# A matmul with a decayed running sum: a quarter of the weights by another queue, new engine orders for the first 40 slots, four input buffers

## The chip, the cores and the metric

The kernel runs on one core of a Trainium2 chip. The metric is the device time of that core in microseconds; the kernel before takes 908.82 us (median of three, 908.58 to 909.28). The profiled execution took 909.17 us, of which the profile covers 907.1 us from the first instruction to the last.

## What is computed

```python
B, S, D = (16, 2048, 1024)          # x: B x S x D, w: D x D, decay: D, all float32
xw = x @ w
out[:, 0, :] = xw[:, 0, :]
for t in range(1, S):
    out[:, t, :] = decay[None, :] * out[:, t - 1, :] + xw[:, t, :]
```

A matrix product of 32768 x 1024 with 1024 x 1024, and then, along the time axis of each batch, a first-order recurrence with one decay factor for each column.

## The kernel before

x is cut into 64 chunks of 512 time steps. GpSimd's queue loads a chunk as bf16 (four transfers, one for each 32 partitions), VectorE turns it in 32x32 blocks so that the summed dimension lies on the partitions ("T"), and ScalarE reorders it into `xt` ("X", "Y"). TensorE multiplies in bf16, eight matmuls (k = 0 to 7) for 128 output columns by 512 time steps. Two chunks make a group; a slot is one group and one of its eight column blocks, so a group has eight slots, and there are 264 slots: the last two chunks are each a group of their own. A slot's result is a "tile" of 128 columns by 1024 time steps, two PSUM banks.

A tile is emptied in one of two ways. Directly: VectorE scans all 1024 steps out of PSUM. Paired: ScalarE copies PSUM ("p") and makes decay times the even steps ("g"), GpSimd adds them to the odd steps ("j"), VectorE scans only 512 steps with the squared decay, ScalarE and GpSimd fill in the other 512 ("h", "c"). `flips` says for which slots the usual choice (every fourth direct) is turned round. Then VectorE transposes the tile back ("B") and SyncE's queue stores four tiles at a time.

The order on each engine is the order in which the program issues. For the first and last slots it is spelled out in `agenda`, a list of letters with numbers; `deeds` says what each letter does. The key -99 is what comes before slot 0.

```python
    def load(c, q, j0=0, j1=NJ):
        b, t0 = chunks[c]
        if c not in xb_of:
            xb_of[c] = ring(sb, "xb", 3, [128, NJ, CQ], BF16)
        pin(nc.gpsimd.dma_start(
            out=xb_of[c][quad(q), j0:j1],
            in_=_ap(x, [[D, P], [P * D, j1 - j0], [1, CQ]],
                    (b * S + t0 + j0 * P) * D + q * CQ)))

    def turn(c, j0=0, j1=NJ, m0=0, m1=M):
        if c not in xw_of:
            xw_of[c] = ring(sb, "xw", 2, [128, M, NJ, P, 2], BF16)
        src = xb_of[c][:, j0:j1].rearrange("p j c -> p (j c)").bitcast(FP32)
        dst = xw_of[c].rearrange("p m j i e -> p (m j i e)").bitcast(FP32)
        pin(nc.vector.transpose(
            out=dst.rearrange("p (m j i) -> p j m i", m=M, i=P)[:, j0:j1, m0:m1],
            in_=src.rearrange("p (j m c) -> p j m c", m=M, c=P)[:, :, m0:m1]))

# ... (cut)
        def pair(self):
            if self.paired:
                self.copy()
                self.odd()
                self.zero()
                self.join()
# ... (cut)
        def scan(self):
            T, n, so = self.T, self.n, self.so
            if self.paired:
                pin(nc.vector.tensor_tensor_scan(
                    out=so[:, 3:T + 2:2],
                    data0=squares[-1][:, n:n + 1].to_broadcast([128, T // 2]),
                    data1=self.xs[:, 1:T:2],
                    initial=0.0 if self.prev is None else self.prev,
                    op0=ALU.mult,
                    op1=ALU.add,
                ))
            else:
                parts = self.ps if isinstance(self.ps, tuple) else (self.ps,)
                size = T // len(parts)
                for i, ps in enumerate(parts):
                    self.run(ps, i * size, size)

# ... (cut)
    room = [ot_tile(2 * NJ).rearrange("p j c -> p (j c)") for _ in range(2)]
    size = M * CH
    stage = {(0, 0, 0): room[0][:, 0:size // 2],
             (0, 0, M // 2): room[0][:, size // 2:size * 3 // 4].bitcast(BF16),
             (0, 1, 0): room[0][:, size:size * 3 // 2].bitcast(BF16),
             (1, 0, 0): room[1][:, 0:size // 2].bitcast(BF16),
             (1, 1, 0): room[1][:, size // 2:size].bitcast(BF16)}

    def load_w(queue, h, e, m0=0, m1=M):
        for q in range(NQ):
            pin(queue.dma_start(
                out=stage[h, e, m0][quad(q)].rearrange("p (m d) -> p m d", m=m1 - m0),
                in_=_ap(w, [[2 * D, P], [2 * P * D, m1 - m0], [1, CH]],
                        (q * CQ + m0 * 2 * P + e) * D + h * CH)))

    def settle(h, e, m, copy):
        m0 = M // 2 if (h, e) == (0, 0) and m >= M // 2 else 0
        src = stage[h, e, m0][:, (m - m0) * CH:(m - m0 + 1) * CH]
        pin(copy(out=wcols[:, 2 * m + e, h],
                 in_=src.rearrange("p (q r i) -> p q r i", q=NQ, r=R)))

# ... (cut)
    load_w(nc.sync, 0, 0, 0, M // 2)          # first quarter of w, float32
# ... (cut)
    def load_part(i):
        load_w(nc.gpsimd, *((0, 0, M // 2, M), (0, 1), (1, 0), (1, 1))[i])

    def part_one(i, copy):
        part(i // 8, copy, i % 4, i % 4 + 1, *halves[i // 4 % 2])

    def settle_one(i, copy):
        settle(i // 8, i // 4 % 2, i % 4, copy)

# ... (cut)
        -99: "M0 M1 U0 U1 M2 M3 U2 U3 W0 w1 L E0 F0 G1 E1 L F2 D G3 E2 F4 L G5 W2 E3 F6 w3 G7 W4 W6 w5 w7 E4 F8 G9 E5 F10 G11 E6 F12 G13 E7 F14 G15 W8 W10 W9 W11",
        0: "P0 L w15 w13",
        1: "L L L S0 C0",
        2: "L P2 P1 w12 S1 L L B0 B1 S2",
        3: "w14 C2 T2",
        4: "S3 P4 X2 Y2 T3 C1",
# ... (cut)
    flips = (0, 1, -19, -18, -16, -11, -8, -6, -3, -2)
# ... (cut)
            for j0, j1 in halves:                    # chunk 0
                for k in (0, 2):
                    for i in range(R):
                        matmul(firsts[i], i, k, xt_of[0], j0 * P, j1 * P)
            for k in (4, 6, 1, 3, 5, 7):
                for i in range(R):
                    matmul(firsts[i], i, k, xt_of[0])
            # ... then chunk 1 in halves of 256 steps
```

The letters of the head: M loads half a chunk, U a quarter of w, E turns a quarter of chunk 0 or 1 (half its steps, half its columns), F and G copy a piece of it into `xt` on VectorE or ScalarE, W and w copy a piece of w into `wsb` on VectorE or ScalarE, D makes the decay factors, L loads a quarter of a later chunk.

Of the kernel before, what the change touches and what calls it, by code (L numbers as in the profile page):

```python
# [10 lines left out]
BF16 = mybir.dt.bfloat16  # L11
# [14 lines left out]
def kernel(  # L26
# [74 lines left out]
    def load(c, q, j0=0, j1=NJ):  # L101
        b, t0 = chunks[c]
        if c not in xb_of:
            xb_of[c] = ring(sb, "xb", 3, [128, NJ, CQ], BF16)
        pin(nc.gpsimd.dma_start(  # L105
            out=xb_of[c][quad(q), j0:j1],
            in_=_ap(x, [[D, P], [P * D, j1 - j0], [1, CQ]],
                    (b * S + t0 + j0 * P) * D + q * CQ)))
# [152 lines left out]
    class Outlet:  # L261
# [7 lines left out]
        def store(self, b, t0):  # L269
# [3 lines left out]
            for i, q in enumerate((0, 2, 1, 3)):  # L273
# [7 lines left out]
    room = [ot_tile(2 * NJ).rearrange("p j c -> p (j c)") for _ in range(2)]  # L281
    size = M * CH
    stage = {(0, 0, 0): room[0][:, 0:size // 2],
             (0, 0, M // 2): room[0][:, size // 2:size * 3 // 4].bitcast(BF16),
             (0, 1, 0): room[0][:, size:size * 3 // 2].bitcast(BF16),
             (1, 0, 0): room[1][:, 0:size // 2].bitcast(BF16),
             (1, 1, 0): room[1][:, size // 2:size].bitcast(BF16)}
# [25 lines left out]
    for q in range(NQ):  # L313
        pin(nc.sync.dma_start(
            out=rows[q * P:q * P + R],
            in_=_ap(decay, [[P, R], [CH, 2], [1, P]], q * CR)))
    cols = const.tile([128, 2, P], FP32, name="cols")

    def load_half(i):
# [35 lines left out]
    def ending(i):  # L355
        b, t0 = chunks[-1]
        nb = TL // 128
        pts = [ring(psp, name, count, [128, R, 128])
               for name, count in (("spare1", 1), ("ps", 3), ("ps", 3), ("spare", 1))]
        wides = [ring(sb, *spot, [128, NQ, R, P])  # L360
                 for spot in (("xb", 3), ("xb", 3), ("xb", 3), ("h", 4))]

        def cross(blocks, rs):
            for i in blocks:
                for r in rs:
                    t = 2 + i * 128
                    pin(nc.tensor.transpose(  # L367
                        out=pts[i][:, r], in_=tiles[r - R].so[:, t:t + 128], identity=ident))

        def leave(i, copy):  # L370
            pin(copy(out=wides[i].rearrange("p q r i -> p r q i"),
                     in_=pts[i].rearrange("p r (q i) -> p r q i", q=NQ)))
            pin(nc.sync.dma_start(
                out=_ap(out, [[D, 128], [1, CH]], (b * S + t0 + i * 128) * D + CH),
                in_=wides[i].rearrange("p q r i -> p (q r i)")))

        cross((0,), range(R))
        cross((1,), range(R))
        cross((2, 3), range(R - 1))
        cross((2, 3), (R - 1,))  # L380
        for i in range(nb):
            leave(i, (nc.scalar.copy, nc.vector.tensor_copy)[i % 2])
# [2 lines left out]
    slots += [([c], n) for c in groups[-1] for n in range(K)]  # L385
    tiles = []

    def turn_and_load(c):
        turn(c)
        if 2 <= c < nch - 3:  # L390
            loads.extend((c + 3, q) for q in range(NQ))

    loads = [(c, q) for c in (2, 3, 4) for q in range(NQ)]
    deeds = {
        "P": lambda s: tiles[s % len(slots)].pair(),
        "S": lambda s: tiles[s % len(slots)].scan(),
        "C": lambda s: tiles[s % len(slots)].complete(),
        "B": lambda s: tiles[s % len(slots)].back(),
        "T": turn_and_load,
        "X": lambda c: part(c, nc.scalar.copy, 0, 2),  # L400
        "Y": lambda c: part(c, nc.scalar.copy, 2, M),
        "x": lambda c: part(c, nc.vector.tensor_copy, 0, 2),
# [21 lines left out]
        "L": lambda i: load(*loads.pop(0)) if loads else None,  # L424
    }
    agenda = {
        -99: "M0 M1 U0 U1 M2 M3 U2 U3 W0 w1 L E0 F0 G1 E1 L F2 D G3 E2 F4 L G5 W2 E3 F6 w3 G7 W4 W6 w5 w7 E4 F8 G9 E5 F10 G11 E6 F12 G13 E7 F14 G15 W8 W10 W9 W11",
        0: "P0 L w15 w13",
        1: "L L L S0 C0",
        2: "L P2 P1 w12 S1 L L B0 B1 S2",  # L430
        3: "w14 C2 T2",
        4: "S3 P4 X2 Y2 T3 C1",
        5: "",
        6: "L L P5 L B3 L L S4 L S5 B2 C3 X3 Y3 C4 T4",
        7: "P6 C5 S7 X4 S6",
        8: "C7 C6 L d P8 B4 B7 B6",
        9: "B5 P9",
        10: "L S8 P10 C8 T5 X5 L S9",
        11: "L L S11 L C9 Y4 S10 C10 B8",
        12: "",  # L440
        13: "B11 P12 B10 B9 Y5 S12 P13 C12",
        14: "L P14 T6 S13 C13 L Y6 L",
        15: "L S15 L S14 C14",
        16: "B13 B12 B15 B14 P16 X6",
        -20: "z-20",
        -19: "p-20 g-20",
        -18: "j-20 S-19 S-20 k-19 B-19",
# [15 lines left out]
        -2: "S-3 S-4",  # L463
        -1: "S-2 h-4 c-4 a-1 b-1 V",
    }
    flips = (0, 1, -19, -18, -16, -11, -8, -6, -3, -2)
    later = {10: ["Y4"]}
    for c in range(5, nch):
        first = c // 2 * K
        ahead = (7, 6, 4) if c % 2 else (11, 10, 8)  # L470
        for letter, a in zip("TXY", ahead):
            later.setdefault(first - a, []).append(f"{letter}{c}")

    def usual(s):
        paired = [t.paired for t in tiles]
# [25 lines left out]
    for step, (g, n) in enumerate(slots):  # L501
# [7 lines left out]
        if step == 0:  # L509
# [1 line left out]
            firsts = [ps[:, 0:TL] for ps in heads] + [spares[0]]  # L511
            seconds = [ps[:, TL:T] for ps in heads] + [spares[1]]
            for j0, j1 in halves:
                for k in (0, 2):
                    for i in range(R):
                        matmul(firsts[i], i, k, xt_of[0], j0 * P, j1 * P)
            for k in (4, 6, 1, 3, 5, 7):
                for i in range(R):
                    matmul(firsts[i], i, k, xt_of[0])
            for k0 in range(0, K, 4):  # L520
# [6 lines left out]
        if step < R:  # L527
            ps = heads[n] if n < 3 else tuple(spares)
        else:
            if len(g) == 2 or n % R < 3:  # L530
                ps = ring(psp, "ps", 3, [128, T])
            else:
                ps = ring(psp, "spare", 1, [128, TL])
# [1 line left out]
            if step < K:  # L535
                todo.sort(key=lambda kl: kl[0] % 2)
            elif step == K:
                todo.sort(key=lambda kl: kl[1])
            if left == -1:
                ps = tuple(both[:, t:t + TL // 2] for t, both in zip(  # L540
                    (0, TL // 2), (ps, ring(psp, "ps", 3, [128, TL]))))
# [44 lines left out]
```

## Time and profile before

| what | value |
|---|---|
| median of three | 908.82 us |
| span of the profile | 907.1 us |
| TensorE clock granted | 1.000 |
| VectorE, ScalarE, GpSimd busy | 829.7, 680.3, 655.5 us |
| GpSimd's queue (loads, cast to bf16) | 68.96 MB |
| SyncE's queue (stores, first quarter of w) | 134.76 MB |
| HBM read and written | 138.42 and 134.22 MB |

Busy time of an engine is not its worth on the path: TensorE's matmuls are pipelined, and in the profile they show as busy for 377 ns each though one starts about every 216 ns. In the group lines and the timeline, a row is: start and length in us, engine, line of the kernel, operation, what it writes and reads, count, and in brackets the idle time before it with what ended that.

### The profile page before, as it was taken

How to read it: one execution, taken by the hardware profiler on the slowest of the kernel's cores; microseconds unless marked ns; L12 is line 12 of the kernel's file. 1: busy time of each engine (PE TensorE's matmuls, PEld its weight loads, DVE VectorE, ACT ScalarE, POOL GpSimd, SP SyncE). 2: the span in 40 equal slices, each digit the busy share in tenths (PEclk: the TensorE clock that was granted, in tenths of full speed). 3: DMA queues.
4: the chain of work that ended last, by engine and by line, in shares of the span. 5: the costliest groups of instructions: out<-in, count | busy, mean ns of one | idle time of the engine just before them, and what ended most of it. 6: DMA issues, size and time to landing. Idle time of an engine off the chain costs nothing.

```text
span 907.1 us, 12011 instructions
## 1 busy us (share of the span) xinstructions
PE 895.3 (99%) x4187; PEld 409.9 (45%) x4187; DVE 829.7 (91%) x620; ACT 680.3 (75%) x940; POOL 655.5 (72%) x754
## 2 busy tenths in 40 slices
PE   7999999999999999999999999999999999999998
PEld 3544444444444444444444444444444444444444
DVE  4999999999999999999999999999999999999998
ACT  3787887877777778778778777787787787787743
POOL 7777978777777777677686776777777777776632
PEclk9999999999999999999999999999999999999999
DMA  9999999999999999999999999999999999999868
GB/s 163 180 226 237 215 217 249 250 251 254 253 250 243 225 230 234 224 228 232 224 234 221 232 228 226 238 226 225 236 227 228 224 238 223 223 229 217 177 144 237
DMA packets 402605, 204.48 MB, mean 225 GB/s; under 512 B 8817, under 2 KB 401777, under 8 KB 402545
## 3 DMA queue, kind: packets, MB, share of 16 engines
q1 hardware_dynamic: 265200, 134.76, 60.1%
q0 software_dynamic: 137344, 68.96, 56.7%
q8 instruction: 32, 0.52, 0.2%
q14 instruction: 29, 0.23, 0.1%
HBM read 138.42 MB, written 134.22 MB: 301 GB/s over the span
## 4 chain that ended last, share of the span: by engine, by line
PE 94%; DMA 2%; ACT 1%; DVE 1%; POOL 1%; issue 0%; DVEq 0%; POOLq 0%
PE ps L126 93%; DMA xb<-in_x_dram 1%; ACT xt L123 1%; PE spare L126 1%; DMA ot<-in_w_dram 1%; DVE so L216 0%; POOL ot L291 0%; ACT h L164 0%; ACT xs L178 0%; POOL xb L105 0%; DVE ot L253 0%; DVE so L196 0%; PE spare L367 0%; DVE wsb L299 0%; PE ps L367 0%
## 5 line engine op out<-in xcount | busy, mean ns | idle before, releaser
L126 PE MATMUL ps<-xt,wsb 128*128 128x512 bf16 (+1 forms) x4086 | 878.0, 377 | 5.1 <-DVE xt L123 2.8
L126 PEld LDWEIGHTS <-wsb 128*128 128x128 bf16 x4144 | 405.3, 98 | 485.7 <-issue 4.8
L191 POOL TENSOR_TENSOR xs<-h,xs 128x512 f32<-128x512 f32 (+1 forms) x188 | 240.8, 1281 | 200.4 <-ACT h L164 96.4
L178 ACT COPY xs<-ps 128x1024 f32<-128x1024 f32 (+1 forms) x188 | 187.7, 998 | 156.4 <-PE ps L126 154.6
L253 DVE STREAM_TRANSPOSE ot<-so 128x1024 f32<-128x1024 f32 (+1 forms) x260 | 299.7, 1191 | 0.8
L241 POOL TENSOR_TENSOR so<-h,xs 128x512 f32<-128x512 f32 (+1 forms) x188 | 240.0, 1277 | 38.1 <-ACT h L164 21.4
L123 ACT COPY xt<-xw 128x2048 bf16<-128x2048 bf16 (+1 forms) x132 | 240.7, 1825 | 9.8 <-DVE xw L115 9.8
L105 POOL DMA_DIRECT2D xb<-in_x_dram x264 | 174.4, 662 | 1.9 <-POOLq L570 0.9
L164 ACT ACTIVATE h<-so,dec 128x512 f32<-128x512 f32 (+1 forms) x188 | 144.2, 767 | 29.5 <-DVE so L196 26.0
L115 DVE STREAM_TRANSPOSE xw<-xb 128x2048 f32<-128x2048 f32 (+1 forms) x70 | 147.4, 2105 | 6.8 <-DMA xb<-in_x_dram 6.8
L196 DVE TENSOR_TENSOR_SCAN so<-spare,keep,xs 128x512 f32<-128x512 f32 (+1 forms) x96 | 119.4, 1244 | 28.2 <-POOL xs L191 27.9
L196 DVE TENSOR_TENSOR_SCAN so<-spare,xs 128x512 f32<-128x512 f32 x88 | 107.5, 1222 | 27.8 <-POOL xs L191 24.9
L164 ACT ACTIVATE h<-ps,dec 128x512 f32<-128x512 f32 (+1 forms) x188 | 129.0, 686 | 0.0
L216 DVE TENSOR_TENSOR_SCAN so<-dec,ps 128x1024 f32<-128x1024 f32 x35 | 79.0, 2260 | 0.6 <-ACT h L164 0.6
L216 DVE TENSOR_TENSOR_SCAN so<-dec,keep,ps 128x1024 f32<-128x1024 f32 (+1 forms) x36 | 77.1, 2143 | 0.1
L245 ACT COPY keep<-so 128x1 f32<-128x1 f32 x136 | 25.6, 188 | 12.4 <-DVE so L216 12.4
L187 ACT COPY so<-keep 128x1 f32<-128x1 f32 x96 | 18.3, 190 | 1.9 <-DVE ot L253 1.9
L126 PE MATMUL spare<-xt,wsb 128*128 128x512 bf16 (+1 forms) x58 | 12.3, 328 | 0.0
L185 POOL MEMSET so<- 128x1 f32 x92 | 10.7, 116 | 1.1 <-ACT keep L245 1.1
L291 POOL DMA_DIRECT2D ot<-in_w_dram x16 | 8.7, 543 | 3.3 <-DMA xb<-in_x_dram 1.8
L309 PE MATMUL spare<-idle 128*128 128x512 bf16 x27 | 7.6, 451 | 2.3 <-ACT idle L307 2.3
L299 ACT COPY wsb<-ot 128x512 bf16<-128x512 bf16 x7 | 4.0, 616 | 5.5 <-DMA ot<-in_w_dram 5.5
(32 smaller groups left out, 32.9 us busy)
## 6 DMA issues: line engine op xcount, KB each, us to landing
out_dram<-ot SPq DMA_DIRECT2D x248, 512.0 KB, 10.5
xb<-in_x_dram POOLq DMA_DIRECT2D x248, 256.0 KB, 7.7
out_dram<-ot SPq DMA_DIRECT2D x12, 256.0 KB, 4.3
xb<-in_x_dram POOLq DMA_DIRECT2D x16, 128.0 KB, 5.5
ot<-in_w_dram POOLq DMA_DIRECT2D x12, 128.0 KB, 5.0
out_dram<-xb SPq DMA_DIRECT2D x3, 256.0 KB
ot<-in_w_dram SPq DMA_DIRECT2D x4, 128.0 KB, 3.4
ot<-in_w_dram POOLq DMA_DIRECT2D x4, 64.0 KB, 4.5
```

The lines of the kernel that those rows point to most:

```text
L105: pin(nc.gpsimd.dma_start(out=xb_of[c][quad(q), j0:j1], in_=_ap(x, [[D, P], [P * D, j1 - j0], [1, CQ]], (b * S + t0 + j0 * P) * D + q * CQ)))
L115: pin(nc.vector.transpose(out=dst.rearrange("p (m j i) -> p j m i", m=M, i=P)[:, j0:j1, m0:m1], in_=src.rearrange("p (j m c) -> p j m c", ...
L123: pin(copy(out=xt_of[c][:, m0:m1, :, j0 * P:j1 * P], in_=src))
L126: pin(nc.tensor.matmul(out=ps[:, t0:t1] if ps.shape[1] >= t1 else ps, lhsT=wsb[:, k, n].rearrange("p q i -> p (q i)"), rhs=xt[:, k // 2, k ...
L164: pin(nc.scalar.activation(out=h, in_=src, func=mybir.ActivationFunctionType.Copy, scale=dec[:, self.n:self.n + 1]))
L178: pin(nc.scalar.copy(out=self.xs, in_=self.ps))
L191: pin(nc.gpsimd.tensor_tensor(out=odds, in0=self.g, in1=odds, op=ALU.add))
L196: pin(nc.vector.tensor_tensor_scan(out=so[:, 3:T + 2:2], data0=squares[-1][:, n:n + 1].to_broadcast([128, T // 2]), data1=self.xs[:, 1:T:2 ...
L216: pin(nc.vector.tensor_tensor_scan(out=so[:, t + 2:t + 2 + size], data0=dec[:, n:n + 1].to_broadcast([128, size]), data1=ps, initial=befor ...
L241: pin(nc.gpsimd.tensor_tensor(out=self.so[:, 2:T + 2:2], in0=self.h, in1=self.xs[:, 0:T:2], op=ALU.add))
L245: pin(nc.scalar.copy(out=self.keep, in_=self.so[:, self.T + 1:self.T + 2]))
L253: pin(nc.vector.transpose(out=outlet.ot[:, :, c0:c0 + P], in_=self.so[:, 2 + t0:2 + t0 + nj * P].rearrange("p (i t) -> p i t", t=P)))
```

## The change

The second quarter of w (even rows, first half of the columns, upper half of the summed dimension) is loaded by SyncE's queue as float32, as the first quarter is, and no longer by GpSimd's queue with a cast to bf16; the room for it in SBUF was there. In return the third quarter stands right behind chunk 0 in GpSimd's queue. Chunk 0 is multiplied in four k by halves of its time steps and not two, so that the first 32 matmuls need only even rows of w. The orders of all engines are spelled out for slots 0 to 41 and not only 0 to 16, other tiles are direct, chunk 2 is turned and chunk 3 is turned in two pieces, and slots 8 and 9 use chunk 2 for both before either uses chunk 3. The input has four buffers and not three, and loads run four chunks ahead. All this is meant to let TensorE run without gaps from an early time on.

```diff
--- before.py
+++ after.py
@@ -101,7 +101,7 @@
     def load(c, q, j0=0, j1=NJ):
         b, t0 = chunks[c]
         if c not in xb_of:
-            xb_of[c] = ring(sb, "xb", 3, [128, NJ, CQ], BF16)
+            xb_of[c] = ring(sb, "xb", 4, [128, NJ, CQ], BF16)
         pin(nc.gpsimd.dma_start(
             out=xb_of[c][quad(q), j0:j1],
             in_=_ap(x, [[D, P], [P * D, j1 - j0], [1, CQ]],
@@ -281,7 +281,7 @@
     room = [ot_tile(2 * NJ).rearrange("p j c -> p (j c)") for _ in range(2)]
     size = M * CH
     stage = {(0, 0, 0): room[0][:, 0:size // 2],
-             (0, 0, M // 2): room[0][:, size // 2:size * 3 // 4].bitcast(BF16),
+             (0, 0, M // 2): room[0][:, size // 2:size],
              (0, 1, 0): room[0][:, size:size * 3 // 2].bitcast(BF16),
              (1, 0, 0): room[1][:, 0:size // 2].bitcast(BF16),
              (1, 1, 0): room[1][:, size // 2:size].bitcast(BF16)}
@@ -314,6 +314,7 @@
         pin(nc.sync.dma_start(
             out=rows[q * P:q * P + R],
             in_=_ap(decay, [[P, R], [CH, 2], [1, P]], q * CR)))
+    load_w(nc.sync, 0, 0, M // 2, M)
     cols = const.tile([128, 2, P], FP32, name="cols")
 
     def load_half(i):
@@ -358,7 +359,7 @@
         pts = [ring(psp, name, count, [128, R, 128])
                for name, count in (("spare1", 1), ("ps", 3), ("ps", 3), ("spare", 1))]
         wides = [ring(sb, *spot, [128, NQ, R, P])
-                 for spot in (("xb", 3), ("xb", 3), ("xb", 3), ("h", 4))]
+                 for spot in (("xb", 4), ("xb", 4), ("xb", 4), ("h", 4))]
 
         def cross(blocks, rs):
             for i in blocks:
@@ -385,18 +386,28 @@
     slots += [([c], n) for c in groups[-1] for n in range(K)]
     tiles = []
 
-    def turn_and_load(c):
-        turn(c)
-        if 2 <= c < nch - 3:
-            loads.extend((c + 3, q) for q in range(NQ))
-
-    loads = [(c, q) for c in (2, 3, 4) for q in range(NQ)]
+    def turn_half(half):
+        def act(c):
+            if half == 0:
+                turn(c, 0, NJ, 0, 2)
+            else:
+                turn_and_load(c, 2)
+        return act
+
+    def turn_and_load(c, m0=0):
+        turn(c, 0, NJ, m0, M)
+        if 2 <= c < nch - 4:
+            loads.extend((c + 4, q) for q in range(NQ))
+
+    loads = [(c, q) for c in (2, 3, 4, 5) for q in range(NQ)]
     deeds = {
         "P": lambda s: tiles[s % len(slots)].pair(),
         "S": lambda s: tiles[s % len(slots)].scan(),
         "C": lambda s: tiles[s % len(slots)].complete(),
         "B": lambda s: tiles[s % len(slots)].back(),
         "T": turn_and_load,
+        "t": turn_half(0),
+        "u": turn_half(1),
         "X": lambda c: part(c, nc.scalar.copy, 0, 2),
         "Y": lambda c: part(c, nc.scalar.copy, 2, M),
         "x": lambda c: part(c, nc.vector.tensor_copy, 0, 2),
@@ -424,24 +435,49 @@
         "L": lambda i: load(*loads.pop(0)) if loads else None,
     }
     agenda = {
-        -99: "M0 M1 U0 U1 M2 M3 U2 U3 W0 w1 L E0 F0 G1 E1 L F2 D G3 E2 F4 L G5 W2 E3 F6 w3 G7 W4 W6 w5 w7 E4 F8 G9 E5 F10 G11 E6 F12 G13 E7 F14 G15 W8 W10 W9 W11",
-        0: "P0 L w15 w13",
-        1: "L L L S0 C0",
-        2: "L P2 P1 w12 S1 L L B0 B1 S2",
-        3: "w14 C2 T2",
-        4: "S3 P4 X2 Y2 T3 C1",
-        5: "",
-        6: "L L P5 L B3 L L S4 L S5 B2 C3 X3 Y3 C4 T4",
-        7: "P6 C5 S7 X4 S6",
-        8: "C7 C6 L d P8 B4 B7 B6",
-        9: "B5 P9",
-        10: "L S8 P10 C8 T5 X5 L S9",
-        11: "L L S11 L C9 Y4 S10 C10 B8",
-        12: "",
-        13: "B11 P12 B10 B9 Y5 S12 P13 C12",
-        14: "L P14 T6 S13 C13 L Y6 L",
-        15: "L S15 L S14 C14",
-        16: "B13 B12 B15 B14 P16 X6",
+        -99: "M0 M1 U1 M2 M3 U2 U3 W0 w1 D W2 w3 E1 E0 G2 G3 F1 F0 E2 E3 G4 G5 F7 F6 W6 w7 W4 W5 E5 E4 G10 F11 G9 F8 E6 E7 L G12 F13 L G15 F14",
+        0: "L W9 w11 L W8 W10 L",
+        1: "S0 L",
+        2: "L p1 z1",
+        3: "L w13 S2 w15 k0 L w14 w12 g1",
+        4: "L B0 k2 j1 B2 p4 L S1 L g4",
+        5: "j4 t2 k1 h1 u2 L X2 c1 S3 Y2 z4 L",
+        6: "L L B1 k3 p5 B3 p6 z5 z6 L",
+        7: "g6 S4 g5 L j6 t3 h4 k4 u3 c4 X3 S6 L Y3 L T4 j5 h6 k6 p7 S5 z7 c6 g7",
+        # ... (slots 8 to 39 cut)
+        40: "S39 h38 k38 c38 B37 p40 g40 z40 j40 k39 B38 B39 L L",
+        41: "p41 g41 z41 j41 S40 h40 c40 L L",
         -20: "z-20",
         -19: "p-20 g-20",
         -18: "j-20 S-19 S-20 k-19 B-19",
@@ -463,13 +499,15 @@
         -2: "S-3 S-4",
         -1: "S-2 h-4 c-4 a-1 b-1 V",
     }
-    flips = (0, 1, -19, -18, -16, -11, -8, -6, -3, -2)
-    later = {10: ["Y4"]}
+    flips = (0, 2, 7, 8, 13, 15, 16, 19, 20, 21, 25, 27, 30, 31, 32, 35, -19, -18, -16, -11, -8, -6, -3, -2)
+    later = {}
+    begun = {"T": 14, "X": 13, "Y": 13}
     for c in range(5, nch):
         first = c // 2 * K
         ahead = (7, 6, 4) if c % 2 else (11, 10, 8)
         for letter, a in zip("TXY", ahead):
-            later.setdefault(first - a, []).append(f"{letter}{c}")
+            if c >= begun[letter]:
+                later.setdefault(first - a, []).append(f"{letter}{c}")
 
     def usual(s):
         paired = [t.paired for t in tiles]
@@ -511,10 +549,10 @@
             firsts = [ps[:, 0:TL] for ps in heads] + [spares[0]]
             seconds = [ps[:, TL:T] for ps in heads] + [spares[1]]
             for j0, j1 in halves:
-                for k in (0, 2):
+                for k in (0, 2, 4, 6):
                     for i in range(R):
                         matmul(firsts[i], i, k, xt_of[0], j0 * P, j1 * P)
-            for k in (4, 6, 1, 3, 5, 7):
+            for k in (1, 3, 5, 7):
                 for i in range(R):
                     matmul(firsts[i], i, k, xt_of[0])
             for k0 in range(0, K, 4):
@@ -527,7 +565,9 @@
         if step < R:
             ps = heads[n] if n < 3 else tuple(spares)
         else:
-            if len(g) == 2 or n % R < 3:
+            if step == K + 1:
+                ps = nexts
+            elif len(g) == 2 or n % R < 3:
                 ps = ring(psp, "ps", 3, [128, T])
             else:
                 ps = ring(psp, "spare", 1, [128, TL])
@@ -535,7 +575,14 @@
             if step < K:
                 todo.sort(key=lambda kl: kl[0] % 2)
             elif step == K:
-                todo.sort(key=lambda kl: kl[1])
+                todo = []
+                nexts = ring(psp, "ps", 3, [128, T])
+                for l in range(len(g)):
+                    for i, both in enumerate((ps, nexts)):
+                        for k in range(K):
+                            matmul(both[:, l * TL:(l + 1) * TL], n + i, k, xt_of[g[l]])
+            elif step == K + 1:
+                todo = []
             if left == -1:
                 ps = tuple(both[:, t:t + TL // 2] for t, both in zip(
                     (0, TL // 2), (ps, ring(psp, "ps", 3, [128, TL]))))
```

## The prediction

> **What bounds the kernel now.** I read the page first, then the stretches of the first 100 us, then TensorE's waits, then the timeline of the head. The page:
>
> ```profile
> span 907.1 us, 12011 instructions
> ...
> PE 895.3 (99%) x4187; PEld 409.9 (45%) x4187; DVE 829.7 (91%) x620; ACT 680.3 (75%) x940; POOL 655.5 (72%) x754
> ...
> PE 94%; DMA 2%; ACT 1%; DVE 1%; POOL 1%; issue 0%; DVEq 0%; POOLq 0%
> ```
>
> TensorE has 94% of the chain that ended last. Busy alone proves little, so I use the rate: the chain has one unbroken piece, 3640 matmuls in 785.79 us from 92.42 us, that is 215.9 ns for 128x512. The whole product is 4096 of these (64 chunks, 8 column blocks, 8 parts of the sum), or 884.3 us. The last of them ends at 900.68 us in the chain, so TensorE lost 16.4 us before or between matmuls; after it come 6.4 us of ending. Only those 22.8 us are to be had, 2.5% of the span, and the change leaves the agenda of the ending as it was. So the 16.4 us are the subject. By stretches (engine, busy us, count; then clock, DMA share, GB/s):
>
> ```profile
> 0.00:10.00 10.00, 7.68 (x28) 3.10 (x29) 2.02 (x6) 2.63 (x4) 7.37 (x17) 1.00 0.91 146
> 10.00:20.00 10.00, 6.91 (x38) 3.57 (x38) 5.03 (x13) 3.60 (x7) 8.43 (x16) 1.00 1.26 171
> 20.00:30.00 10.00, 9.44 (x75) 7.13 (x73) 9.14 (x14) 4.23 (x8) 7.99 (x14) 1.00 1.32 195
> 30.00:40.00 10.00, 8.68 (x41) 3.86 (x41) 9.44 (x8) 8.14 (x12) 6.48 (x9) 1.00 1.45 196
> 40.00:50.00 10.00, 9.88 (x47) 4.39 (x46) 10.00 (x7) 9.73 (x12) 7.73 (x10) 1.00 1.05 132
> 100.00:200.00 100.00, 100.00 (x465) 45.37 (x464) 94.12 (x68) 78.89 (x107) 77.49 (x86) 1.00 1.26 238
> ```
>
> The loss is over by about 50 us; later TensorE is full. Two more things are seen: DMA is the full engine up to 40 us, and VectorE is full from 30 to 50 us. TensorE's waits:
>
> ```profile
> PE ps L126 <- DVE xt L123: 2.8, 3, 2.0
> PE spare L309 <- ACT idle L307: 2.3, 1, 2.3
> PE ps L126 <- ACT wsb L299: 1.3, 1, 1.3
> PE ps L126 <- DVE wsb L299: 0.6, 1, 0.6
> PE ps L126 <- DVE so L216: 0.2, 1, 0.2
> ```
>
> The first real matmul starts at 9.95 us; the waits after it sum to 4.9 us. What stands behind them, in the timeline:
>
> ```profile
> 9.95 0.49 PE L126 MATMUL ps<-xt,wsb 128*128 128x256 bf16 x3
> ...
> 16.64 0.50 DVE L299 COPY wsb<-ot 128x512 bf16<-128x512 bf16 x2 [2.20 <-DMA ot<-in_w_dram]
> 19.73 0.71 DVE L115 STREAM_TRANSPOSE xw<-xb 128x512 f32<-128x512 f32 x1 [2.58 <-DMA xb<-in_x_dram]
> 28.24 1.14 ACT L299 COPY wsb<-ot 128x512 bf16<-128x512 bf16 x2 [3.37 <-DMA ot<-in_w_dram]
> 31.53 18.80 PE L126 MATMUL ps<-xt,wsb 128*128 128x512 bf16 x85 [1.32 <-ACT wsb L299]
> ```
>
> Each long wait of VectorE or ScalarE in the head is for a transfer. The trace's landings of single transfers come almost evenly, one 128 KB transfer of GpSimd's queue each 0.65 us: chunk 0 first half 8.60, second half 11.44, second quarter of w 12.78, third quarter (odd rows) 16.52, chunk 1 halves 19.60 and 22.31, the two late quarters 24.92 and 28.14, chunk 2 at 33.49, chunk 3 at 38.84. So the head is bound by DMA order and rate, then by VectorE and ScalarE emptying PSUM.
>
> **What the Trainium skill says.** DMA: Bandwidth & Descriptors, Issuing engines are not separate DMA queues: transfers of several issuing engines interleave on the same 16 DMA engines, and another issuer saves only issue time. The trace agrees in kind: while SyncE's first four transfers land (3.47 to 6.46 us) only two of GpSimd's do. The same page, Queues, rings and completion order, has each DMA engine take turns between queues, so the moved quarter won't wait behind x but share with it. VectorE: DVE Perf Modes, The perf-mode tier table, has a float32 copy at half the rate of a bf16 one at best; here 427 against 293 ns, so the float32 quarter costs only tenths more. TensorE: Matmul & The Clock Gate, Back-to-back issue gap, gives about 216 ns for an isolated 512-column matmul but 131 ns in a stream; this stream runs at 215.9, and the measurement decides: no faster TensorE is hidden here.
>
> **Part 1: the second quarter of w.** It leaves GpSimd's queue, where it took 12.78 - 11.44 = 1.34 us. GpSimd keeps eight transfers open, and waited four times (1.8 us) to issue these. Because of that the third quarter was issued late: it first landed 1.32 us after its forerunner and last 1.16 us after, instead of 0.65 each, 1.2 us of holes. Now it is issued right behind chunk 0, so I take both back: -2.5 us. Against it stand four 128 KB float32 transfers on SyncE's queue, issued after decay from about 4 us. The page's queue table gives that queue 134.76 MB in 60.1% of 907 us, or 0.53 us for 128 KB: 2.1 us at most. GpSimd's queue didn't run full from 5.5 to 8 us, so some fits in holes; I charge 1.3. Chunk 0 thus lands about 1.3 us later, at 9.9 and 12.7, and everything from the third quarter on 1.2 us earlier: third quarter 15.3, chunk 1 at 18.4 and 21.1, late quarters 23.7 and 26.9.
>
> **Part 2: chunks 0 and 1.** For chunk 0 VectorE now turns both halves (2 x 0.71), then copies the second 32 columns, then the first (2 x 0.43), and the first matmul needs the last of these: 9.9 + 2.3 = 12.2 us, 2.2 later than before. The moved quarter's cast (its last landing about 10 us) stands before the turning and can add 0.5. Then 32 half matmuls (k = 0, 2, 4, 6) run almost without a gap, 3.5 us, to about 16.0, where before they ended at 16.4 and waited for the third quarter until 17.0. Sixteen odd ones take 3.45: 19.5. Chunk 1 needs 18.4 + 2.3 = 20.7 (before: 20.95); its 64 halves took 7.15 us from 20.95 to 28.1, so they end at 27.85. Slot 4's even matmuls need 1.73 us: 29.6. The last quarter lands at 26.9; ScalarE does tile 1's copy (1.0, to 27.0), two weight copies, a small one, two more (4 x 0.57 + 0.1), the needed one last: 29.4. Before, this point was reached at 31.53. Gain there: 1.9 us.
>
> **Part 3: slots 4 to 41.** From slot 5 on TensorE would start slot s at 31.3 + 3.454(s - 5). PSUM has three two-bank tiles, so slot s + 3 waits until tile s is read. Tiles 0, 2, 3, 8, 11, 13 and on are scanned by VectorE directly, 14 of the first 40 where before it was 12. The first tight one is tile 8, needed free at slot 11, 52.0 us. VectorE starts tile 0's scan at 25.1 and has, by start-to-start times in the timeline, three direct scans of two banks 6.6, tile 3 2.35, four half-length scans 4.44, six outgoing transposes at 1.135 6.8, the halves of two x transposes 4.44, one whole 2.21, a small one 0.1: 26.95, to 52.05. There is no slack, and any idle time of VectorE before it delays TensorE. It idled 0.5 us in the comparable piece before (for xb), so I take 0.5 off the gain. The same sum carried on gives slack of about 0.5 at tiles 11 and 13, then 3 us from tile 16 on. Chunk 2 ahead of chunk 3 gives chunk 3's turning 3.45 us more; it is needed at about 45.1, and behind the scalings of slots 5 and 4 ScalarE has it at 44 to 46: met, or nearly. The fourth buffer lets chunk 3 and 4 be loaded before chunk 0's and 1's buffers are all free; VectorE's idle time for xb was 6.8 us in the whole run, none of it on TensorE's path after 50 us. So it is permission for the order, not a gain.
>
> **Sum.** 1.9 - 0.5 = 1.4 us. 908.82 - 1.4 = 907.4 us.
>
> **Rivals.** First, SyncE's float32 transfers take a full share: chunk 0 lands 2 us later, the rest only 0.5 earlier. For it: fast early service of SyncE's queue in the trace. Then slot 5 is reached 1 us earlier and VectorE's lack of slack takes half: 908.3. Second, VectorE becomes the bound in slots 8 to 16, or ScalarE's queue of copies (it was full from 40 to 50 us too) holds PSUM at slots 8 to 11: the gain is eaten and 0.5 to 1.5 more: about 909.5. For it: two more direct scans and no slack by my sum; against it: the new order evidently spaces direct scans, and TensorE can still be behind by 1.9 us at no loss. Third, the holes in DMA close better than I think (late quarters at 26 us) and nothing else bites: 3 us gained, 905.8. A loss beyond 10 us would need a long starvation in slots 12 to 41, where VectorE has 6% and ScalarE 21% free; I see no cause.
>
> **Range and chances.** The middle is 907.4; the rivals span 905.8 to 909.5, and I widen the better side: 904.8 to 909.7. Faster by 2% would need 18 of the 22.8 lost us: 1%. Slower by 2%: 2%. The rest, 97%, is within 2%.
>
> **What would show it.** Right: first real matmul at 12 to 13 us but no 2 us hole after it; third quarter used by 16 us; odd matmuls of slot 4 begin near 29.6; an unbroken stream after, with at most a small wait on a direct scan or ScalarE at slots 8 to 11; 3640-matmul rate still 215.9. Wrong: chunk 1 turned after 19.7 us, a wait of over 1 us in slots 8 to 16, or any wait of TensorE after 60 us.

## The result: slower by 0.35%

The changed kernel took 912.35 us (median; single runs 912.0 to 913.2) against 909.05 us for the kernel before, a ratio of 1.0035 with a 95% interval of 1.0018 to 1.0052. Predicted were 907.4 us and a range of 904.8 to 909.7. The class, within 2%, was right; direction and range were wrong.

### The profile after

First the page of the changed kernel: the span, the engines, and the chain that ended last by engine.

```profile
span 910.1 us, 11923 instructions
...
PE 891.3 (98%) x4113; PEld 411.6 (45%) x4195; DVE 830.7 (91%) x622; ACT 675.9 (74%) x933; POOL 649.2 (71%) x745
...
PE 89%; DVE 5%; DMA 3%; issue 2%; ACT 1%; POOL 0%; DVEq 0%; ACTq 0%; POOLq 0%
```

Against the first fence of the prediction there is one large difference: VectorE now has 5% of the chain, where it had 1%, and TensorE 89%, where it had 94%. (The lower busy time of TensorE is no slower rate: line 126 has 4152 weight loads but only 4070 matmuls, so the trace lost some matmul records; the weight loads are still 215.8 ns apart.) Then the stretches of the head, with the columns as before (the last three are clock, DMA share and GB/s).

```profile
0.00:10.00 10.00, 7.42 (x27) 3.00 (x28) 1.36 (x6) 2.09 (x3) 7.09 (x16) 1.00 0.92 157
10.00:20.00 10.00, 4.17 (x25) 3.20 (x25) 5.99 (x14) 3.58 (x7) 7.08 (x13) 0.66 1.34 193
20.00:30.00 10.00, 9.95 (x77) 7.42 (x76) 5.31 (x11) 3.21 (x6) 7.51 (x13) 1.00 1.27 188
50.00:60.00 10.00, 8.65 (x41) 3.84 (x40) 10.00 (x9) 9.22 (x12) 7.21 (x6) 1.00 1.29 225
```

Two stretches are new: from 10 to 20 us TensorE has a clock of 0.66 and less than half the work of the kernel before (25 matmuls, all of 256 columns; there 38, of which the last 22 have 512), and from 50 to 60 us, where it had been full, it is idle for 1.35 us while VectorE is busy for all ten. TensorE's waits (engine, line, waited for: us in total, times, longest):

```profile
PE ps L126 <- DVE xt L123: 6.1, 1, 6.1
PE spare L309 <- ACT idle L307: 2.3, 1, 2.3
PE ps L126 <- DVE so L216: 1.3, 1, 1.3
PE ps L126 <- ACT xt L123: 0.2, 1, 0.2
```

The six small waits of the kernel before (4.9 us in all) have become one of 6.1 us at the start, one of 1.3 us for a direct scan and one of 0.2 us. The timeline shows what stands behind both.

```profile
13.34 0.43 DVE L299 CAST wsb<-ot 128x512 bf16<-128x512 f32 x1 [4.12 <-DMA ot<-in_w_dram]
13.68 1.29 DVE L115 STREAM_TRANSPOSE xw<-xb 128x512 f32<-128x512 f32 x2
15.82 0.80 PE L126 MATMUL ps<-xt,wsb 128*128 128x256 bf16 x3 [6.12 <-DVE xt L123]
...
50.32 1.18 DVE L196 TENSOR_TENSOR_SCAN so<-squares,xs 128x512 f32<-128x512 f32 x1
50.38 2.21 POOL L241 TENSOR_TENSOR so<-h,xs 128x512 f32<-128x512 f32 x1 [0.57 <-ACT keep L245]
51.42 1.20 DVE L340 TENSOR_TENSOR spare<-dec 128x8 f32<-128x8 f32 x1
...
54.82 2.30 DVE L216 TENSOR_TENSOR_SCAN so<-dec,keep,ps 128x1024 f32<-128x1024 f32 x1
57.17 1.02 PE L126 MATMUL ps<-xt,wsb 128*128 128x512 bf16 x4 [1.30 <-DVE so L216]
```

VectorE stands for 4.12 us at the cast of the moved quarter, because that cast is ahead of chunk 0's turning in its order. (What is called the first and the second quarter of w is an eighth each: GpSimd's queue had carried the second in four transfers of 64 KB as bf16, half the size of its other transfers of w, and SyncE's queue now moves 135.29 MB, 0.53 MB more than before.) Chunk 0's first half had landed at 9.17 us; the moved quarter's four transfers landed at 9.98, 10.92, 12.16 and 13.22. The first real matmul comes at 15.82 us, 5.9 later than before. Three matmuls of 256 columns in 0.80 us there, and 0.49 us in the kernel before: until 18.9 us the first 14 or so ran at half clock. Later, a product of 128 x 8 elements takes VectorE 1.20 us, beside a GpSimd addition of 2.21 instead of 1.30 us, and 1.30 us is what TensorE then waits for tile 8.

The bookkeeping: slot 4 starts at 31.21 us against 28.33 (+2.9); slot 4's own wait of 1.32 us is gone (-1.3); tile 8's wait is new (+1.3). That is 2.9 of the 3.0 us between the two spans. The late start of 5.9 us became only 2.9 by slot 4, since odd rows of w (16.43 us, before 16.52) and chunk 1's first half (18.96, before 19.60) were not later, and TensorE no longer paused for them.

### The profile page after: what moved, and what is told of

It reads as the page before. It is cut to its first block, busy times and chain, and to the rows that moved or that the text cites. A ratio compares the mean times of both kernels' runs of the same rounds, so it can differ in the third digit from the quotient of the medians.

```text
span 910.1 us, 11923 instructions
## 1 busy us (share of the span) xinstructions
PE 891.3 (98%) x4113; PEld 411.6 (45%) x4195; DVE 830.7 (91%) x622; ACT 675.9 (74%) x933; POOL 649.2 (71%) x745
## 3 DMA queue, kind: packets, MB, share of 16 engines
q1 hardware_dynamic: 265520, 135.29, 60.4%
## 4 chain that ended last, share of the span: by engine, by line
PE 89%; DVE 5%; DMA 3%; issue 2%; ACT 1%; POOL 0%; DVEq 0%; ACTq 0%; POOLq 0%
PE ps L126 88%; DMA xb<-in_x_dram 2%; DVE so L216 2%; DVE so L196 1%; PE spare L126 1%; DVE ot L253 1%; DVE xw L115 1%; DMA ot<-in_w_dram 1%; ACT xs L178 0%; ACT h L164 0%; POOL xs L191 0%; ACT xt L123 0%; PE spare L368 0%; DVE spare L340 0%; PE ps L368 0%
## 5 line engine op out<-in xcount | busy, mean ns | idle before, releaser
L178 ACT COPY xs<-ps 128x1024 f32<-128x1024 f32 (+1 forms) x186 | 185.6, 999 | 162.8 <-PE ps L126 155.6
L115 DVE STREAM_TRANSPOSE xw<-xb 128x2048 f32<-128x2048 f32 (+2 forms) x72 | 146.8, 2047 | 3.4 <-DMA xb<-in_x_dram 3.4
L216 DVE TENSOR_TENSOR_SCAN so<-dec,ps 128x1024 f32<-128x1024 f32 x36 | 81.3, 2261 | 3.7 <-PE ps L126 3.1
L216 DVE TENSOR_TENSOR_SCAN so<-dec,keep,ps 128x1024 f32<-128x1024 f32 (+1 forms) x37 | 79.4, 2146 | 0.1
L245 ACT COPY keep<-so 128x1 f32<-128x1 f32 x136 | 25.6, 188 | 16.4 <-DVE so L216 12.2
L126 PE MATMUL spare<-xt,wsb 128*128 128x256 bf16 (+1 forms) x60 | 13.1, 330 | 0.0
```

The lines of the kernel that those rows point to most:

```text
L115: pin(nc.vector.transpose(out=dst.rearrange("p (m j i) -> p j m i", m=M, i=P)[:, j0:j1, m0:m1], in_=src.rearrange("p (j m c) -> p j m c", ...
L126: pin(nc.tensor.matmul(out=ps[:, t0:t1] if ps.shape[1] >= t1 else ps, lhsT=wsb[:, k, n].rearrange("p q i -> p (q i)"), rhs=xt[:, k // 2, k ...
L178: pin(nc.scalar.copy(out=self.xs, in_=self.ps))
L216: pin(nc.vector.tensor_tensor_scan(out=so[:, t + 2:t + 2 + size], data0=dec[:, n:n + 1].to_broadcast([128, size]), data1=ps, initial=befor ...
L245: pin(nc.scalar.copy(out=self.keep, in_=self.so[:, self.T + 1:self.T + 2]))
```

## The experiments

All compare with runs of the kernel before on the same chip, so the ratio is the number to compare. "First" is the first real matmul, "slot 4" its first matmul, "tile 8" TensorE's wait for the direct scan of tile 8 at slot 11 (the kernel before has no such tile; in c it is not direct). Half clock tells whether the profile has half-clock matmuls in the head.

| run | us | ratio (95%) | first | slot 4 | tile 8 | half clock |
|---|---|---|---|---|---|---|
| before | | 1 | 9.95 | 28.33 | | no |
| changed | 912.35 | 1.0035 (1.0018 to 1.0052) | 15.82 | 31.21 | 1.30 | yes |
| a casts later | 912.36 | 1.0033 (1.0021 to 1.0046) | 11.44 | 27.64 | 2.54 | no, but after tile 8 |
| b more empty matmuls | 910.77 | 1.0018 (1.0012 to 1.0025) | 15.44 | 29.37 | 1.30 | no |
| c quarter moved alone | 912.12 | 1.0030 (1.0020 to 1.0040) | 11.05 | 30.08 | | yes |
| d product early | 911.85 | 1.0024 (1.0014 to 1.0033) | 16.14 | 32.20 | 0 | yes |
| e a + d | 908.89 | 0.9988 (0.9980 to 0.9997) | 11.38 | 28.78 | 0 | yes |
| f e + three edits | 909.43 | 0.9994 (0.9986 to 1.0002) | 11.28 | 29.11 | 0 | yes |
| g e, quarter not moved | 908.93 | 0.9990 (0.9982 to 0.9998) | 11.01 | 28.22 | 0 | no |
| i quarter issued earlier | 910.28 | 1.0010 (1.0001 to 1.0018) | 13.70 | 29.15 | 1.30 | yes |
| j i + d + three edits | 909.51 | 1.0000 (0.9986 to 1.0013) | 13.78 | 28.31 | 0 | no |
| k g + three edits | 908.88 | 0.9995 (0.9987 to 1.0003) | 11.43 | 28.05 | 0 | no |
| m b + d | 909.98 | 1.0005 (0.9996 to 1.0013) | 15.83 | 29.76 | 0 | no |

My theory after the result had three parts: the cast's place in VectorE's order made the late start; the late start cost half clock on top; the small product made most of the wait for tile 8. The rival was that VectorE and the transfers set the time whatever happens before.

### a: the casts of the moved quarter behind chunk 0's first half

```diff
- W0 w1 D W2 w3 E1 E0 G2 G3 F1 F0 E2 E3 ...
+ W0 w1 D E1 E0 G2 G3 F1 F0 W2 w3 E2 E3 ...
```

> The changed kernel, but VectorE and ScalarE cast the moved quarter of w behind chunk 0's first half instead of ahead of it. Theory 1 (in the changed kernel VectorE stands for 4.1 us at the cast of a quarter that lands at 13.2 us, so the first matmul comes at 15.8 instead of 9.95 us): first half of chunk 0 has landed at 9.2, so the first matmul comes at about 11.6 us, slot 4 starts near 28.5 instead of 31.2, and the time falls by 2.7 us to about 909.6. Theory 2 (the head's transfers and then VectorE emptying PSUM set the time, whatever happens before 20 us): the first matmul moves, slot 11 waits for longer, and the time stays within 0.7 us of 912.3.

The head did what theory 1 said, slot 4 from 27.64 instead of 31.21 us; the time did what theory 2 said. The timeline of this run at slot 11:

```profile
47.68 1.29 POOL L241 TENSOR_TENSOR so<-h,xs 128x512 f32<-128x512 f32 x1 [0.54 <-ACT keep L245]
47.76 2.29 DVE L196 TENSOR_TENSOR_SCAN so<-squares,xs 128x512 f32<-128x512 f32 x1
49.31 1.83 POOL L191 TENSOR_TENSOR xs<-h,xs 128x512 f32<-128x512 f32 x1 [0.34 <-POOL so L241]
49.98 1.20 DVE L340 TENSOR_TENSOR spare<-dec 128x8 f32<-128x8 f32 x1
...
55.73 1.78 PE L126 MATMUL ps<-xt,wsb 128*128 128x512 bf16 x5 [2.54 <-DVE so L216]
```

Two VectorE instructions are stretched by 1.1 us each (2.29 for 1.18, 1.20 for 0.15), so TensorE's wait doubles; and five matmuls in 1.78 us after it are nearly all at half clock again. In both profiles it is the later of two neighbours that is stretched: here the addition of 47.68 us keeps its 1.29 us and the scan that begins 0.08 us after it takes 2.29; in the changed kernel the scan began 0.06 us first, kept its 1.18 us, and the addition took 2.21. The 3.6 us gained at slot 4 are gone: 0.6 us for the last quarter's cast, 1.2 more at tile 8, some 1.5 at half clock, and small waits.

### b: TensorE kept busy

```diff
- for _ in range(27):   # empty matmuls
+ for _ in range(53):
```

> The changed kernel with 53 instead of 27 empty matmuls at the start, which fill TensorE until about 15.4 us; nothing else changes. Theory 1: the idle 6.1 us cost more than themselves, because the first 14 half matmuls after them ran at half clock (214 ns each instead of 107, 1.5 us in all): first matmul still at 15.8 us, clock 1.0 from 10 to 20 us, time 1.5 us lower, about 910.9. Theory 2 (the matmuls from 15.8 to 21 us wait for odd rows of w and chunk 1 in any case): no change, 912.3.

As theory 1: the stretch from 10 to 20 us has the clock at 1.00, slot 4 starts 1.84 us earlier though the first matmul is only 0.38 us earlier, and the ratio falls by 0.0017, 1.5 us. Half clock was about half of the loss.

```profile
10.00:20.00 10.00, 9.77 (x61) 5.89 (x61) 6.22 (x14) 3.74 (x7) 7.40 (x13) 1.00 1.35 200
15.44 0.49 PE L126 MATMUL ps<-xt,wsb 128*128 128x256 bf16 x3 [0.18 <-DVE xt L123]
```

The empty matmuls compute nothing that is used; before and after are the same in this.

### c: the moved quarter alone, in the kernel before

```diff
- (0, 0, M // 2): room[0][:, size // 2:size * 3 // 4].bitcast(BF16),
+ (0, 0, M // 2): room[0][:, size // 2:size],
+ load_w(nc.sync, 0, 0, M // 2, M)      # behind decay
- M0 M1 U0 U1 M2 M3 U2 U3
+ M0 M1 U1 M2 M3 U2 U3
```

> The kernel before with only the second quarter of w moved to SyncE's queue as float32; all orders, three buffers and the k halves as before. Theory 1 (the moved transfer is harmless where no engine stands before it in order): the second half of chunk 0 lands near 14 instead of 11.4 us and the late quarters 0.3 us earlier, and the point where slot 4 goes on stays bound by the last quarter: 909.0, within 0.7 of before. Theory 2 (the moved transfer itself makes the change slower, by sharing the DMA engines with chunk 0): slot 4 starts 2 us later or more, 911 or above.

Theory 1 was wrong here, theory 2 right in the time (slot 4 came 1.75 us later, where it had said 2 or more): the moved transfer alone makes the kernel before as slow as the whole change does. Its orders do not put the cast ahead of chunk 0, so the first matmul is at 11.05; but then this follows:

```profile
11.05 0.49 PE L126 MATMUL ps<-xt,wsb 128*128 128x256 bf16 x3
...
15.69 0.80 PE L126 MATMUL ps<-xt,wsb 128*128 128x256 bf16 x3 [3.60 <-DVE xt L123]
...
49.02 2.32 PE L126 MATMUL ps<-xt,wsb 128*128 128x512 bf16 x10 [1.07 <-ACT h L164]
```

Chunk 0's second half landed at 14.34 us instead of 11.44, 2.9 later, and after 3.6 us of waiting TensorE was at half clock. Slot 4's own wait is shorter in return (0.27 us, before 1.32), so its odd matmuls begin only 0.7 us late, at 32.24 us. But the engines that empty PSUM stay 1.7 us late: ScalarE's "h" that TensorE waits for at 49.02 us begins at 48.28 us, before at 46.60, and that wait is new, as is one of 0.68 us at 94.8 us for a direct scan. So the moved transfer has a cost of its own; the cast's place in the new order only decides where it is paid.

### d: the small product behind tile 3's scan

```diff
- 5: "... X2 c1 S3 Y2 z4 L",          9: "d B4 k5 h5 j7",
+ 5: "... X2 c1 S3 d Y2 z4 L",        9: "B4 k5 h5 j7",
```

> The changed kernel, but VectorE's small product of the squared decay (128x8), which took 1.20 us at 51.4 us beside a GpSimd addition of 2.2 instead of 1.3 us, is made right behind tile 3's scan, where GpSimd only issues loads. Theory 1 (this product held VectorE for 1.1 us and so makes most of TensorE's 1.30 us wait for tile 8 at slot 11): the product takes 0.15 us, the wait falls to about 0.2 us, the time by 1.1 us to 911.2. Theory 2 (two more direct scans leave VectorE short by that much in any case): the wait stays above 1 us and the time at 912.3.

Mechanism as theory 1: the product takes 0.17 us and TensorE has no wait for tile 8.

```profile
42.40 0.17 DVE L340 TENSOR_TENSOR spare<-dec 128x8 f32<-128x8 f32 x1
PE ps L126 <- DVE xt L123: 5.6, 1, 5.6
PE ps L126 <- ACT xt L123: 0.4, 1, 0.4
```

The ratio fell by 0.0011, 1.0 us, near the 1.1 us expected, but the intervals overlap, so this run alone does not show a gain. In its profile half clock lasted until 20.5 us instead of 18.9, and slot 4 came 1.0 us later, which hides the gain there. Run m takes that away.

### m: b and d together

> The changed kernel with 53 empty matmuls and with the squared decay right behind tile 3's scan; VectorE still stands at the cast of the moved quarter. Theory 1 (half clock and the product beside GpSimd's addition are two separate losses, and the product's gain was hidden when it was moved alone because the half clock lasted 1.7 us longer in that profile): first matmul at 15.4, slot 4 at 29.4, no wait for tile 8, and a time 1.1 below the run with empty matmuls alone, about 909.7, level with the kernel before. Theory 2 (the product only filled a wait that some other engine sets): a wait of about 1 us at slots 8 to 11 stays and the time is that of the run with empty matmuls alone.

```profile
PE ps L126 <- ACT xt L123: 0.4, 1, 0.4
```

That is the only wait on line 126 left. The ratio is 1.0005 against 1.0018 for b, 1.2 us lower, and level with the kernel before, with VectorE still standing at the cast and the first matmul at 15.83 us. So the loss is, within the intervals, two things: half clock (0.0017) and the product beside GpSimd's addition (0.0013). Their sum is surer than its division: m's interval lies wholly below that of the changed kernel, b's and d's overlap it.

### e, f: the casts and the product, then three edits more

f adds to e: last quarter cast in the order of use, tile 8's scan ahead of tile 6's transpose, 34 empty matmuls.

```diff
- 3: "L w13 S2 w15 k0 L w14 w12 g1",  10: "X4 B6 c5 S8 Y4 L B5",
+ 3: "L w12 S2 w13 k0 L w14 w15 g1",  10: "X4 c5 S8 B6 Y4 L B5",
```

> The changed kernel with both edits: the casts of the moved quarter behind chunk 0's first half, and the squared decay right behind tile 3's scan. Theory 1 (with the first edit alone TensorE reached slot 11 early and then lost all of it, 2.5 us waiting for tile 8 and some 1.5 at half clock after that wait; VectorE was late because a half-length scan took 2.29 instead of 1.18 us and the small product 1.20 instead of 0.15, both with two operands in SBUF and beside a GpSimd addition): scans read the squares from PSUM early, none is stretched, the wait at slot 11 falls to 0.3 to 0.6 us, the clock stays 1.0, and the time is about 908.7, 3.6 less than the changed kernel. Theory 2 (VectorE has too much work before tile 8 whatever GpSimd does): the wait stays above 1.5 us, the time above 911.

> The same two edits, and three more: the last quarter of w is cast by ScalarE in the order in which TensorE uses it (k = 1, 3, 5, 7), tile 8's scan stands ahead of tile 6's outgoing transpose on VectorE, and seven more empty matmuls fill TensorE until 11.2 us. Theory 1: the 0.56 us wait in slot 4 goes, the scan of tile 8 ends 1.1 us earlier, slot 11 starts without a wait near 52.7 us, and the time is about 907.9, below the kernel before by 1. Theory 2 (the next engine takes it up: ScalarE's copies of chunk 3 or PSUM held at slots 9 and 10): within 0.4 us of the run with two edits.

e came out as expected in time, 0.0047 of ratio below the changed kernel, and is the first version faster than the kernel before, by 0.12% (0.03 to 0.20%). Two details missed: there is no wait for tile 8 at all, and the clock did not stay up:

```profile
14.05 0.75 PE L126 MATMUL ps<-xt,wsb 128*128 128x256 bf16 x3 [1.64 <-DVE wsb L299]
48.55 81.78 PE L126 MATMUL ps<-xt,wsb 128*128 128x512 bf16 x369 [0.76 <-ACT xt L123]
```

After 0.61 and 1.64 us of idle time its matmuls are at half clock until 17.6 us. This profile is of e's slowest execution, 910.89 us. The granted clock of each execution tells of the others: four of e's 13 have 0.999 or 1.000 and took 907.9 to 908.6 us, nine have 0.997 or 0.998 and a median of 909.4. f took the small waits in slot 4 away and still was no better, 909.43 where theory 1 had 907.9 us; its profile too has half clock, from 15.3 to 18.7 us, and its five executions at 0.999 or 1.000 have a median of 908.7, the other eight 909.6. That puts about 1 us on the clock in both, but it is a sorting of few executions and no experiment: in g the three with the lower clock were not slower. f's last store was issued 0.35 us earlier than that of the kernel before, yet its span ended 0.7 us later: the end after the last issue varied from 3.4 to 4.4 us between these profiles, so differences below a microsecond between single profiles mean little.

### g, k: the quarter back in GpSimd's queue

g is e with the three lines of c undone; k adds the three edits of f, with 32 empty matmuls.

> The changed kernel with the same two edits, but the second quarter of w loaded by GpSimd's queue as bf16 behind chunk 0, as in the kernel before. Theory 1 (the moved quarter holds up chunk 0's second half by 2.7 us but brings chunk 1 forward by about 1 us, and with the casts in place only chunk 1 counts): first matmul near 11 us, chunk 1 used near 21.8, slot 4 from 28.9 instead of 27.6; time about 0.7 above the run with the quarter moved. Theory 2 (the moved quarter is a loss in any order): 1 us or more below that run.

> The run with the quarter back in GpSimd's queue and two edits, with the order of the last quarter's casts, tile 8's scan first and five more empty matmuls added. Theory 1 (its waits for the quarter, landing at 12.6, and for chunk 1 at 19.0 to 20.3 stay): slot 4 near 28.2, slot 8 waiting up to 0.5 us for chunk 3's copies, 0.8 to 1.0 us below the kernel before, and 0.5 above the run with SyncE first. Theory 2 (the quarter's queue does not matter once the orders fit): the two runs agree within 0.3 us.

```profile
28.22 18.29 PE L126 MATMUL ps<-xt,wsb 128*128 128x512 bf16 x82
```

g equals e in time (0.9990 and 0.9988): neither theory's difference appeared. Its chunk 1 was used at 21.11 us and its slot 4 started at 28.22, near the expected 21.8 and 28.9. e had a head that could have been 1 us shorter, as a's 27.64 shows, and in its profile lost that to half clock. k is told apart neither from g nor from j (0.9995 and 1.0000), which theory 1 had 0.5 us below k. So with the orders mended the move of the quarter brought nothing measurable, and what remains of the change (its orders with the product moved, its direct tiles, its four buffers) is worth about 0.1% at most; these parts were not tried one by one.

### i, j: the quarter issued ahead of decay

```diff
  load_w(nc.sync, 0, 0, 0, M // 2)
+ load_w(nc.sync, 0, 0, M // 2, M)      # and no longer behind decay
- W0 w1 D W2 w3 E1 E0 G2 G3 F1 F0 E2
+ W0 w1 W2 w3 E1 E0 G2 G3 F1 F0 D E2
```

> The changed kernel with SyncE issuing the second quarter of w directly behind the first, ahead of decay, so that none of its transfers waits for an earlier landing; the decay factors are made behind chunk 0's first half on VectorE. Theory 1 (the quarter landed at 13.2 us mostly because it shares the DMA engines with x; its own waits for issue gave 1.9 us of that): it lands near 10.5, chunk 0's first half near 10.5 instead of 9.2, first matmul near 13 us, a shorter gap and little half clock: time about 910. Theory 2 (issue waits don't matter): it lands within 1 us of 13.2 and the time stays at 912.

> The changed kernel with SyncE issuing the second quarter of w directly behind the first, decay factors behind chunk 0's first half, the squared decay behind tile 3's scan, the last quarter cast in the order of use, tile 8's scan ahead of tile 6's transpose, and 42 empty matmuls, which fill TensorE until about 13 us. Theory 1 (with the quarter early, no engine waiting for it and no half clock, only chunk 1's landing sets the head): first matmul near 13.5 us at full clock, one stream from there, slot 4 near 27.9, no wait over 0.5 us after it: 1.5 us below the kernel before. Theory 2 (VectorE or ScalarE gives it back at slots 8 to 11, as it did with the casts alone): a wait of 1 us or more there, within 0.5 us of the kernel before.

i did as theory 1 says: the quarter landed at 11.06 instead of 13.22, first matmul 13.70, 910.28 us; tile 8's 1.30 us stayed, as the product was untouched. But chunk 0's first half came at 10.85 instead of 9.17 us: the transfers only change places. In j, with d and f's three edits (42 empty matmuls) and the clock at 1.0, TensorE waited 0.17 us in slot 4, 0.58 for PSUM at slot 8 and 0.76 for chunk 3's copies, together about what its head had won, and the time is that of the kernel before (12 executions from 907.7 to 910.1 us, and one of 915.9). That is nearer theory 2.

## Why the prediction was wrong

**What bounds the kernel.** Right. All differences lie before 60 us, at an unchanged rate of 215.8 ns, and the fixed sum of 884 us leaves no room for 2%.

**Part 1, "I charge 1.3".** The first failed term. Chunk 0's second half came at 14.19 us, 2.75 later than before, not 1.3 (its first half at 9.17, 0.6 later), and the moved quarter at 13.2, not "about 10". I took the four float32 transfers at the rate SyncE's queue has by its share of the run, and let some fit in holes; in fact, after the 9.17 us of chunk 0's first half, one transfer of x landed up to 12.9 us, beside three of the quarter. I had named the sharing and did not carry it through: the moved transfers are slowed too, from 2.7 us from issue to landing for the first of w's to 6.0 us for the first of the second quarter. A line that I misread pointed there: in the kernel before, one of GpSimd's transfers (5.80 us), not two, landed while SyncE's first four did. The other side of the sum, "-2.5 us", was not too large: from chunk 0's last landing to that of the third quarter it took 2.24 us instead of 5.08, a gain of 2.84. But against it stood 2.75 and not 1.3, so the third quarter landed only 0.1 us earlier, chunk 1's halves 0.6 and 0.4 and the late quarters 0.4 and 0.3, where I had said 1.2. The first rival, "SyncE's float32 transfers take a full share", is what happened, and its "0.5 earlier" was a good figure; what it makes of the time was not.

**Part 2, "can add 0.5".** The second failed term. I saw that the cast stands ahead of the turning, and priced it with the wrong landing: VectorE stood there for 4.12 us. First matmul 15.82, predicted 12.2; slot 4 at 31.21, predicted 27.85. Slot 4's odd matmuls, which I had at 29.6, began at about 32.9, before at 31.53; with the casts moved (a) at 30.10, and without half clock (b) at about 31.1.

**Not in the sum at all: the clock.** I took 3.5 us for the first 32 half matmuls; they took 5.2. The Trainium skill (TensorE: Matmul & The Clock Gate, Part 1: The HAM clock gate) states it: TensorE falls to half clock after an idle window of about 3.4 us, windows that run free of the kernel. The traces agree on the half clock and on the windows: each half-clock stretch before 70 us lasted 3.41 or 6.83 us. They differ on "idle", and there the measurement decides: a window need not be idle throughout. In the 13 profiles together nine windows between 8 and 70 us had 1.91 to 3.41 us without a matmul, and half clock followed each of them; the most idle window that full clock followed had 1.79 us. f (first two lines) and a (last two) show both sides:

```profile
11.86:15.28 3.42, 1.50 (x13) 0.96 (x11) 1.80 (x4) 1.29 (x3) 2.38 (x5) 1.00 1.30 199
15.28:18.69 3.41, 3.41 (x16) 2.43 (x17) 1.70 (x6) 1.09 (x2) 3.23 (x6) 0.50 1.43 191
...
8.50:11.91 3.41, 1.62 (x11) 0.82 (x10) 2.65 (x7) 1.14 (x2) 1.56 (x3) 1.00 1.30 229
11.91:15.32 3.41, 1.70 (x15) 1.14 (x13) 1.89 (x4) 1.37 (x3) 2.38 (x5) 1.00 1.29 199
```

With TensorE busy for 1.50 us of a window the next one is at half clock; with 1.62 and 1.70 it is not. So what counted was the idle time summed over a window: the 2.54 us of a and the 3.3, 3.6, 5.6 and 6.1 us of i, c, d and the changed kernel filled most of one or more, the two shorter waits of e and of f fell into one, and the 1.97 us of the kernel before were split between two (1.46 us idle in the first, 1.02 in the second). I read a clock of 1.000 in the kernel before and did not ask what a 2 us longer gap would do to it.

**Part 3, "no slack".** Right in kind and place: tile 8 at slot 11, named as the first tight one. Wrong in the term "a small one 0.1": it was 1.20 us. From tile 0's scan to the end of tile 8's took 28.32 us, 26.95 by my sum. The Trainium skill has the likely reason (SBUF — State Buffer, Who interferes with whom): a VectorE instruction with two inputs in SBUF and a GpSimd instruction that reads SBUF exclude each other. The trace fits: the scan of 50.32 us reads squares and xs in SBUF, the addition started beside it lasts until 52.6 us, and the product, two inputs in SBUF, ends with it. In d, e, g and m, with the product made while GpSimd issued loads, it took 0.17 us, and of the four such scans after it up to 60 us, which then read the squares from PSUM, none took over 1.19. That moving it removes the wait is shown; that the lock is the mechanism was not tried by itself. Of the signs of being wrong, one came, the wait of over 1 us in slots 8 to 16 (1.30 us at slot 11); chunk 1 was turned at 19.09 us, before 19.7, and TensorE had no wait after 60 us.

**The rivals and the range.** The second rival, "about 909.5", had the right place and was the nearest. I let each rival stand alone. The result is the first and the second together with a cost in neither, and the widening went to "the better side", the wrong one.

Left open: why one execution of j took 915.9 us and three of b 913.3 to 914.3, at clocks of 0.995 and 0.998 where their others have 0.999 or 1.000, and how much e and f would win with a clock kept steady and the quarter moved; f's seven empty matmuls filled the gap before the first matmul, not the two after it.

## What to carry to other kernels

When a transfer moves to another queue, work out anew when each transfer lands, with the share that each takes from the other, before pricing anything behind it; then look at where its consumer stands in its engine's order, because everything after it inherits the landing. A gap in TensorE's work is to be priced with the half clock that can follow it, and short gaps close to each other count together. And a small VectorE instruction on a full engine is to be priced with what GpSimd is doing at that moment, not by its size.

## What the runs showed of the hardware that was not expected

A 128 x 8 product on VectorE took 0.14 to 0.17 us or 1.20 us, by what GpSimd did meanwhile, and a 512-step paired scan between 1.18 and 2.29. A wait of 2.5 us in the middle of a full stream (a, slot 11) was enough for about 3.4 us at half clock after it, and so were two shorter waits with 1.91 us together in one window of 3.41 us (f). Starting TensorE 4 us earlier (a) or not (the changed kernel) made no difference to the time that these runs can tell; 26 matmuls whose results nobody uses made 1.5 us.
